# Odd mixer of a two-layer diffusion backbone: decays of head 0 under the query products, output gates by Exp and Ln, gate tiles between the values

## The chip, the cores and the metric

The kernel runs on one core of one Trainium2 chip. The metric is the device time of one execution in microseconds (us), lower is better. A core has TensorE (matrix products, PE in the profile, with its weight loads as PEld), VectorE (DVE), ScalarE (ACT), GpSimd (POOL), SyncE (SP, which issues most loads here) and 16 DMA engines. The engines run apart from each other and wait for each other by semaphores; each executes its own instructions in the order in which the program lists them.

## The reference, cut to what matters

Two layers; each is a SwiGLU FFN, a token mixer and a second FFN. 256 context tokens and 256 latent tokens of width 1024 pass through the same weights. The mixer of the second (odd) layer is a bidirectional gated linear attention (GLA) with 4 heads. Only its latent output is needed, since it is the last layer.

```python
def odd_mixer(hx, hc, w_in, w_out, w_gate, b_gate, norm_g, need_ctx):
    px = _split(hx @ w_in, ODD_SPLITS)     # q 512, k 512, v 1024, r 1024, low rank 32
    pc = _split(hc @ w_in, ODD_SPLITS)
    def heads(p):
        q = p[0].reshape(b, t, GLA_HEADS, GLA_K) * (GLA_K ** -0.5)
        ...
        lr_f, lr_b = jnp.split(p[4], 2, axis=-1)
        def decay(lr, d):
            z = (lr @ w_gate[d] + b_gate[d]).astype(jnp.float32)
            return (jax.nn.log_sigmoid(z) / GLA_TAU).reshape(b, t, GLA_HEADS, GLA_K)
        return (q, k, v), (decay(lr_f, 0),), (decay(lr_b, 1),)
    def merge(o, r):
        y = rms_norm(o, norm_g).reshape(b, t, -1) * jax.nn.silu(r)
        return y.astype(dt) @ w_out
    ...
    ox, oc = bidir_scan(gla_scan, qkv_x..., st0, need_ctx)   # chunks of 64, both directions
    return merge(ox, px[3]), ...
```

silu(r) = r * sigmoid(r) = r * exp(-ln(1 + exp(-r))).

## The kernel before, in words

**Products.** Weights come from HBM in fp32, 1 MB a load (a `raw` tile of 8 x 128 rows x 256 columns, three buffers, issued by SP). Each half of 128 columns is split by `split` into a high part `whi` (ScalarE, L122) and a low part `wlo` (VectorE, L123), two buffers of each. The activations are kept as `hh` and `hl` in the same manner. A product is then three matmuls (L148 high x high, L149 high x low, L150 low x high, in `mm3`) for each of 8 slices of the inner dimension. With 256 latent columns a half is 24 matmuls. `proj_fm` does this for keys, queries and output gates, with the features on the partitions, a PSUM bank `mm` per half (two banks in all), and an `emit` function that takes the result out of the bank. `proj_rows` makes the values of one head, with the tokens on the partitions: 96 matmuls (L636 to L638), both `mm` banks, and two copies by ScalarE (L640).

**The odd mixer** in program order: keys of all heads (`proj_first`); the eight tiles `sr` of the output gate, silu(r) (L1282, one ScalarE Silu per tile); the load of ScalarE's table for Ln and Exp (`table(LN_EXP)`, L109); `low_rank`, which makes the two 16-wide inputs `lr` of the decay gates; two pairs of queries (`q_pair`, L1122); the decays of head 0; then a loop over the heads. In the loop of head h come: the values of h (`proj_rows`); the scores of h (`scores`); the decays of head h + 1; the states of h (`states`); the output of h (`head_out`, which multiplies by `sr[2h]` and `sr[2h+1]`, L1273).

**`decays(h, d)`** for one head and one direction: a product `pz` of 512 columns (L1152); log sigmoid of it by a min and subtract on VectorE (L1155, L1159) and Abs, Exp, Ln on ScalarE (L1156 to L1158); two cumulative sums on VectorE (L1166 or L1172, L1169 or L1173); three Exp on ScalarE (L1178 to L1180); then products on VectorE: `kd` (L1182), `qe` (L1184), `ke` (L1185), `q2` (L1192), `ku` (L1198), `dec` (L1203); small copies on POOL; three transposes on TensorE (`ptg`, L1206 and L1207) and a copy `kt` (L1209).

**What sets the order on the engines.** The program is written in Tile. At build time a planner runs through the program with its own costs and gives each engine, at each time, the ready instruction that stands earliest in the program; a tile that must share a buffer waits until that buffer is free. So an engine's order is fixed before the run, and it isn't the written order: values of the next head, for instance, run on TensorE between the steps of the decays. On the chip each engine keeps to this order even when an instruction's input comes later than the planner thought.

Of the kernel before, what the change touches and what calls it, by code (L numbers as in the profile page):

```python
# [12 lines left out]
AF = mybir.ActivationFunctionType  # L13
ALU = mybir.AluOpType
# [15 lines left out]
LAT = slice(T, TT)  # L30
# [6 lines left out]
def backbone_kernel(  # L37
# [28 lines left out]
    nc = tc.nc  # L66
# [5 lines left out]
    def mm_bank(name):  # L72
        return pm.tile([P, 512], F32, tag="mm", name=name)
# [20 lines left out]
    one_t = cp.tile([P, 1], F32, name="one_t")  # L94
# [13 lines left out]
    def table(name):  # L108
        tc.keep_in_program_order(nc.scalar.preload_act_table_set(name))  # L109
# [4 lines left out]
    def load(view3):  # L114
        raw = wp.tile([P, 2048], F32, tag="raw", name="raw")
        a, b = view3.shape[1], view3.shape[2]
        r3 = raw[:, : a * b].rearrange("p (a b) -> p a b", a=a)
        nc.sync.dma_start(r3, view3)
        return r3
# [5 lines left out]
    def split(r3):  # L125
        a, b = r3.shape[1], r3.shape[2]
        hi = wp.tile([P, 1024], F32R, tag="whi", name="whi", bufs=2)
        lo = wp.tile([P, 1024], F32R, tag="wlo", name="wlo", bufs=2)
        hi3 = hi[:, : a * b].rearrange("p (a b) -> p a b", a=a)
        lo3 = lo[:, : a * b].rearrange("p (a b) -> p a b", a=a)  # L130
        split_into(hi3, lo3, r3)
        return hi3, lo3
# [8 lines left out]
    def rows(w, c0, n, k0=0, nk=KC):  # L141
        return w[k0 * P : (k0 + nk) * P, c0 : c0 + n].rearrange("(k p) n -> p k n", p=P)

    def half(r3, m):
        return split(r3[:, :, m * P : m * P + P])
# [6 lines left out]
    def gemm_h(ps, w, sl, at=None):  # L152
        at = at or sl
        for k in range(KC):
            wh, wl = (t[k] if isinstance(t, list) else t[:, k] for t in w)
            mm3(ps[:, sl], wh, wl, hh[k][:, at], hl[k][:, at], k == 0, k == KC - 1)
# [446 lines left out]
    def proj_fm(w, c0, n, emit, sl=BOTH):  # L603
        for mp in range(n // 2):
            r3 = load(rows(w, c0 + mp * 256, 256))
            for m in range(2):
                wt = half(r3, m)
                ps = mm_bank("ps_fm")
                gemm_h(ps, wt, sl)
                emit(2 * mp + m, ps)  # L610
# [13 lines left out]
    def proj_rows(w, c0, dst, col):  # L624

        r3 = load(rows(w, c0, 256))
        ps = [mm_bank("ps_v") for _ in range(2)]
        for i in range(2):
            wh, wl = split(r3[:, 4 * i : 4 * i + 4])
            for t in range(4):  # L630
                o = ps[t // 2][:, (t % 2) * T : (t % 2) * T + T]
                for k4 in range(4):
                    k = 4 * i + k4
                    ah, al = (a[k][:, t * P : t * P + P] for a in (hh, hl))

                    nc.tensor.matmul(o, lhsT=ah, rhs=wh[:, k4], start=k == 0 and t % 2 == 0, stop=False)  # L636
                    nc.tensor.matmul(o, lhsT=ah, rhs=wl[:, k4], start=False, stop=False)  # L637
                    nc.tensor.matmul(o, lhsT=al, rhs=wh[:, k4], start=False, stop=k == KC - 1 and t % 2 == 1)  # L638
        for a in range(2):
            nc.scalar.copy(dst[:, 2 * a : 2 * a + 2, col : col + T], ps[a].rearrange("p (t n) -> p t n", t=2))  # L640

    def out_split(k, src, sl):
        nc.scalar.copy(hh[k][:, sl], src)
        nc.vector.tensor_tensor(hl[k][:, sl], src, hh[k][:, sl].bitcast(F32), ALU.subtract)
# [18 lines left out]
    def out_weights(w, m0, spares):  # L663

        r = [load(rows(w, (m0 + 2 * a) * P, 256)) for a in range(2)]
        return [
            half(r[t // 2], t % 2) if sp is None else split_spare(r[t // 2], t % 2, sp) for t, sp in enumerate(spares)
        ]
# [6 lines left out]
    def taker(pool, slots, twice=()):  # L675
        slots = list(slots)

        def new():
            tag = slots.pop(0)
            return pool.tile([P, TT], F32R, tag=tag, name="wspare", bufs=2 if tag in twice else 1)  # L680

        return new
# [389 lines left out]
    def odd_mixer(nxt):  # L1072
        w_in, w_out = odd_w_in[0], odd_w_out[0]
# [10 lines left out]
        def t2k(tag, name, bufs=1):  # L1084
            return mp_.tile([P, TT], F32, tag=tag, name=name, bufs=bufs)
# [29 lines left out]
        sr = [mp_.tile([P, T], F32, name=f"sr{e}") for e in range(8)]  # L1115
# [3 lines left out]
        def q_pair(i):  # L1119
            proj_fm(  # L1120
                w_in, 256 * i, 2,
                lambda m, ps: nc.scalar.activation(qT[2 * i + m], ps[:, LAT], AF.Copy, scale=float(P) ** -0.5), LAT,  # L1122
            )

        def low_rank():

            for d in range(2):
                for i in range(3):
                    r0 = 32 * i + 16 * d
                    nc.sync.dma_start(wgraw[d][r0 : r0 + 16], gla_w_gate[0, d])  # L1130
                nc.scalar.copy(wg[d], wgraw[d])
                mid = slice(32, 64)
                nc.vector.tensor_tensor(wg[d][mid], wgraw[d][mid], wg[d][mid].bitcast(F32), ALU.subtract)
            lraw = mp_.tile([P, KC, 32], F32, name="lraw")
            nc.sync.dma_start(lraw, rows(w_in, 3072, 32))
            lw = wp.tile([P, 1024], F32R, tag="whi", name="lw", bufs=2)[:, 0:512].rearrange("p (k r) -> p k r", k=KC)
            nc.scalar.copy(lw[:, :, 0:32], lraw)
            nc.vector.tensor_tensor(lw[:, :, 32:64], lraw, lw[:, :, 0:32].bitcast(F32), ALU.subtract)
            psl = mm_bank("psl")
            for k in range(KC):  # L1140
                for i, a in enumerate((hh[k], hl[k])):
                    nc.tensor.matmul(psl[0:64], lhsT=lw[:, k], rhs=a, start=k + i == 0, stop=k + i == KC)
            low, s = t2k("la0", "low")[0:32], t2k("la1", "lrs")[0:32]
            nc.scalar.copy(low, psl[32:64])
            nc.vector.tensor_tensor(s, psl[0:32], low, ALU.add)
            nc.scalar.copy(lr[0:32], s)
            nc.vector.tensor_copy(lr[32:64], s)
            nc.vector.tensor_tensor(lr[64:96], s, lr[0:32].bitcast(F32), ALU.subtract)
# [95 lines left out]
        def states(h, d, kt, dec):  # L1244

            c0 = d
            hv = slice(h * T, h * T + T)
            pS = bank_d(d, "pSg")
            for t in range(2):
                nc.tensor.matmul(pS[:, :T], lhsT=kt[:, t * P : t * P + P], rhs=v[:, t, hv], start=t == 0, stop=t == 1)  # L1250
            nc.tensor.matmul(pS[:, T:], lhsT=kt[:, 2 * P : 3 * P], rhs=v[:, 2 + c0, hv], start=True, stop=True)
            st = mp_.tile([P, 2, T], F32, tag=f"st{d}", name="st", bufs=2)
            nc.scalar.copy(st[:, c0], pS[:, :T])
            nc.vector.scalar_tensor_tensor(st[:, 1 - c0], st[:, c0], dec, pS[:, T:], ALU.mult, ALU.add)
            return st
# [23 lines left out]
            lambda name: bank_d(0, name),  # L1279
            taker(mp_, ("la0", "la1", "ex0", "ex1", "kd0", "kd1", "spare", "ong")),  # L1280
        )
        proj_fm(w_in, 2048, 8, lambda m, ps: nc.scalar.activation(sr[m], ps[:, LAT], AF.Silu), LAT)  # L1282
        table(LN_EXP)
        low_rank()
        q_pair(0)
        q_pair(1)
        dirs = {0: [decays(0, d) for d in range(2)]}
        gate = md[:, 1, 40:48, :]
        st = STREAMS[1]

        def tiles(bank):

            p = [bank("ps_y") for _ in range(2)]
            return [p[t // 2][:, t % 2 * T : t % 2 * T + T] for t in range(4)]

        for h in range(4):
            proj_rows(w_in, 1024 + 256 * h, v, h * T)
            if h == 3:
                for k in range(4):
                    out_split(k, yo[k], LAST)  # L1300
                new = taker(mp_, [f"gk{i}" for i in range(4)] + ["la0", "la1", "ex0", "ex1"])
                ws = out_weights(w_out, 0, (None, None, new, new))
            am = scores(dirs[h])
            if h < 3:
                dirs[h + 1] = [decays(h + 1, d) for d in range(2)]
            sts = [states(h, d, *dirs[h][d][4:6]) for d in range(2)]
            head_out(h, am, [dirs[h][d][2] for d in range(2)], sts)
        ps = tiles(mm_bank)
# [10 lines left out]
        ps = tiles(bank_c)  # L1319
# [10 lines left out]
    with tc.tile_pool(name="plast", bufs=1, space=PSUM) as pa, tc.tile_pool(name="last", bufs=1) as fp:  # L1330

        def bank(name):
            return pa.tile([P, 512], F32, tag="ff", name=name, bufs=4)
# [27 lines left out]
        ps = [[bank("ps_l") for _ in range(2)] for _ in range(2)]  # L1361
# [94 lines left out]
```

## Time and profile before

| | us |
|---|---|
| median of 3 runs | 1787.75 (1784.91 to 1788.17) |
| the profiled execution | 1790.07 |
| its span, first to last instruction | 1788.4 |
| granted TensorE clock, mean | 0.995 |
| keys' last product, first of the gates | about 1440.9 |
| gate products (`sr`) | 1440.9 to 1463.9 |
| low rank, queries | 1463.7 to 1479.2 |
| head 0's decays beside its values | 1479.2 to 1493.8 |
| loops of heads 0 to 3, with outputs | 1493.8 to 1571.1 |

Times in the profile are counted from the span's start. In a table of stretches each row gives the busy time of each engine in that stretch (number of instructions in brackets), then the granted clock of TensorE as a share of full speed. Matmuls are pipelined: one of 256 columns is recorded with 0.28 us, but the next starts 0.12 us later. In the timeline a row gives start, duration, engine, line, operation and tiles, and in square brackets the idle time ahead of it and what ended it.

### The profile page before, as it was taken

What the parts mean: (1) busy time and instruction counts of PE and PEld (TensorE: products, weight loads), DVE (VectorE), ACT (ScalarE), POOL (GpSimd) and SP (SyncE); (2) the same over time, 40 slices, a digit from 0 to 9 for tenths busy, and PEclk for the clock granted to TensorE, in tenths of its full rate; (3) what the DMA queues carried; (4) which work ended last, traced back from release to release, by engine and by line L of the source; (5) the groups of instructions that cost most, each with busy time, mean ns of one, the idle gap of its engine ahead of it and who ended that gap; (6) DMA issues with size and microseconds to landing.
All of it is one profiled execution on the core that took longest, in us unless ns stands there. A gap on an engine that the chain in (4) does not pass through costs nothing.

```text
span 1788.4 us, 24901 instructions
## 1 busy us (share of the span) xinstructions
PE 1748.8 (98%) x10087; PEld 1505.4 (84%) x10087; DVE 1151.9 (64%) x1678; ACT 742.8 (42%) x1286; POOL 106.7 (6%) x172
## 2 busy tenths in 40 slices
PE   7999999999999999999999999999999999999998
PEld 5788888899887798888888898888888998889996
DVE  4677776657668866777753485777533737855555
ACT  3422222247558854222222252222322645654443
POOL 1000000003011111000000010000000200010000
PEclk9999999999999999999999999999999999999999
DMA  9555555544121214455543344555442632236553
GB/s 288 189 166 187 188 165 188 171 130 126 48 71 48 95 48 141 165 187 187 188 149 96 126 146 165 188 189 188 143 149 85 190 118 72 80 109 198 187 195 118
DMA packets 209303, 262.30 MB, mean 147 GB/s; under 512 B 6863, under 2 KB 188662, under 8 KB 209188
## 3 DMA queue, kind: packets, MB, share of 16 engines
q1 hardware_dynamic: 208160, 259.28, 44.4%
q8 instruction: 79, 1.29, 0.3%
q0 software_dynamic: 576, 0.84, 0.2%
q10 hardware_dynamic: 452, 0.59, 0.1%
q14 instruction: 36, 0.29, 0.0%
HBM read 259.64 MB, written 1.05 MB: 146 GB/s over the span
## 4 chain that ended last, share of the span: by engine, by line
PE 84%; DVE 8%; ACT 4%; issue 2%; DMA 2%; POOL 0%; SPq 0%; ACTq 0%; POOLq 0%; DVEq 0%
PE ps_ab L148 15%; PE ps_ab L149 15%; PE ps_ab L150 15%; PE ps_y L148 7%; PE ps_y L150 7%; PE ps_y L149 7%; PE ps_fm L150 2%; PE ps_fm L149 2%; PE ps_fm L148 2%; DVE wlo L123 2%; PE po L911 1%; ACT whi L122 1%; PE ada_ps L193 1%; PE ps_l L1386 1%; PE ps_l L1387 1%
## 5 line engine op out<-in xcount | busy, mean ns | idle before, releaser
L122 ACT CAST whi<-raw 128x1024 fp32r<-128x1024 f32 (+1 forms) x326 | 336.3, 1032 | 824.3 <-PE ps_ab L149 451.2
L123 DVE TENSOR_TENSOR wlo<-raw,whi 128x1024 fp32r<-128x1024 f32 (+1 forms) x326 | 392.5, 1204 | 305.9 <-ACT whi L122 301.3
L149 PE MATMUL ps_ab<-hl,whi 128*128 128x512 f32 (+1 forms) x1360 | 483.6, 356 | 2.6 <-POOL hl L279 2.3
L148 PE MATMUL ps_ab<-hh,whi 128*128 128x512 f32 (+1 forms) x1360 | 484.4, 357 | 1.7 <-ACT whi L122 1.0
L150 PE MATMUL ps_ab<-hh,wlo 128*128 128x512 f32 (+1 forms) x1360 | 482.5, 355 | 1.2 <-DVE wlo L123 1.1
L181 DVE SCALAR_TENSOR_TENSOR acc<-raw_ada,cs,acc 128x1024 f32<-128x1024 f32 x224 | 276.5, 1280 | 48.2 <-DMA raw_ada<-in_ada_w_dram 48.1
L148 PEld LDWEIGHTS ps_ab<-hh,whi 128*128 128x128 f32 x1360 | 255.1, 188 | 44.3 <-ACT whi L122 6.6
L149 PEld LDWEIGHTS ps_ab<-hl,whi 128*128 128x128 f32 x1360 | 255.5, 188 | 39.8 <-POOL hl L279 2.9
L150 PEld LDWEIGHTS ps_ab<-hh,wlo 128*128 128x128 f32 x1360 | 255.4, 188 | 38.7 <-DVE wlo L123 1.8
L150 PE MATMUL ps_y<-gh,wlo 128*128 128x512 f32 (+1 forms) x660 | 229.9, 348 | 0.4
L148 PE MATMUL ps_y<-gh,whi 128*128 128x512 f32 (+1 forms) x660 | 230.0, 348 | 0.0
L149 PE MATMUL ps_y<-gl,whi 128*128 128x512 f32 (+1 forms) x660 | 228.8, 347 | 0.0
L150 PEld LDWEIGHTS ps_y<-gh,wlo 128*128 128x128 f32 x660 | 124.9, 189 | 17.6 <-DVE wlo L123 1.5
L148 PEld LDWEIGHTS ps_y<-gh,whi 128*128 128x128 f32 x660 | 124.9, 189 | 17.0 <-ACT whi L122 1.2
L149 PEld LDWEIGHTS ps_y<-gl,whi 128*128 128x128 f32 x660 | 124.9, 189 | 15.5
L353 DVE TENSOR_TENSOR s<-ps_ab,s 128x512 f32<-128x512 f32 (+1 forms) x88 | 54.7, 622 | 118.0 <-PE ps_ab L150 117.9
L260 POOL TENSOR_TENSOR ssum<-ssum,sq 128x256 f32<-128x256 f32 x25 | 26.2, 1049 | 1103.0 <-ACT sq L258 834.4
L148 PE MATMUL ps_fm<-hh,whi 128*128 128x256 f32 (+1 forms) x256 | 83.9, 328 | 0.0
L150 PE MATMUL ps_fm<-hh,wlo 128*128 128x256 f32 (+1 forms) x256 | 83.5, 326 | 0.0
L149 PE MATMUL ps_fm<-hl,whi 128*128 128x256 f32 (+1 forms) x256 | 83.1, 325 | 0.0
L636 PE MATMUL ps_v<-whi,hh 128*128 128x256 f32 x256 | 74.2, 290 | 1.2 <-ACT mv L640 1.2
L637 PE MATMUL ps_v<-wlo,hh 128*128 128x256 f32 x256 | 74.6, 291 | 0.0
(375 smaller groups left out, 2396.3 us busy)
## 6 DMA issues: line engine op xcount, KB each, us to landing
raw<-in_ffn_w_in_dram SPq DMA_DIRECT2D x84, 1024.0 KB, 5.4
raw_ada<-in_ada_w_dram SPq DMA_DIRECT2D x64, 1024.0 KB, 5.0
raw<-in_ffn_w_out_dram SPq DMA_DIRECT2D x41, 1024.0 KB, 4.9
raw<-in_even_w_in_dram SPq DMA_DIRECT2D x12, 1024.0 KB, 5.4
raw<-in_odd_w_in_dram SPq DMA_DIRECT2D x12, 1024.0 KB, 5.5
raw<-in_ffn_w_out_dram SPq DMA_DIRECT2D x15, 768.0 KB, 4.2
raw_c<-in_ada_w_dram SPq DMA_DIRECT2D x16, 512.0 KB, 7.0
raw<-in_even_w_out_dram SPq DMA_DIRECT2D x4, 1024.0 KB, 5.0
```

The costliest lines, as they stand in the source:

```text
L122: nc.scalar.copy(hi3, r3)
L123: eng.tensor_tensor(lo3, r3, hi3.bitcast(F32), ALU.subtract)
L148: nc.tensor.matmul(ps, lhsT=wh, rhs=ah, start=first, stop=False)
L149: nc.tensor.matmul(ps, lhsT=wh, rhs=al, start=False, stop=False)
L150: nc.tensor.matmul(ps, lhsT=wl, rhs=ah, start=False, stop=last)
L181: nc.vector.scalar_tensor_tensor(ada_acc[i], r3[:, k2], s, ada_acc[i], ALU.mult, ALU.add)
L193: nc.tensor.matmul(ps[32 * j : 32 * j + 32, :256], lhsT=unit_e[:, 2 * (n - first) + i], rhs=acc[i][:, j * 256 : j * 256 + 256], start=n == ...
L260: (nc.gpsimd if i and k < KC - 2 else nc.vector).tensor_tensor(ssum[i][0], ssum[i][0], sq, ALU.add)
L353: nc.vector.tensor_tensor(s[:, sl], ps[1][:, sl], s[:, sl], ALU.mult)
L636: nc.tensor.matmul(o, lhsT=ah, rhs=wh[:, k4], start=k == 0 and t % 2 == 0, stop=False)
L637: nc.tensor.matmul(o, lhsT=ah, rhs=wl[:, k4], start=False, stop=False)
L911: nc.tensor.matmul(po[:, t], lhsT=w[:, kt, (t % 2) * P : (t % 2) * P + P], rhs=v[:, kt, h * P : h * P + P], start=kt == 0, stop=kt == nk - 1,)
```

## The change

The eight gate tiles lose their place after the keys. `emit_sr` makes silu without the Silu table: min(-r, 80) on VectorE, then Exp, Ln(1 + .), Exp(-.) on ScalarE in place, and a last product with r on VectorE, which reads r from the PSUM bank once more. `sr_pair(h)` projects the two tiles of head h. The pair of head 0 comes after the queries, the pair of head h + 1 between the values and the scores of head h. The decays of head 0 are moved ahead of the second pair of queries (they need only the first), and `low_rank` and the load of the Ln and Exp table now follow the keys directly.

```diff
@@ -1122,6 +1122,18 @@
+        def emit_sr(m, ps):
+
+            x, y = ps[:, LAT], sr[m]
+            nc.vector.tensor_scalar(y, x, -1.0, 80.0, ALU.mult, ALU.min)
+            nc.scalar.activation(y, y, AF.Exp)
+            nc.scalar.activation(y, y, AF.Ln, bias=one_t)
+            nc.scalar.activation(y, y, AF.Exp, scale=-1.0)
+            nc.vector.tensor_tensor(y, x, y, ALU.mult)
+
+        def sr_pair(h):
+            proj_fm(w_in, 2048 + 256 * h, 2, lambda m, ps: emit_sr(2 * h + m, ps), LAT)
+
@@ -1279,12 +1291,12 @@
-        proj_fm(w_in, 2048, 8, lambda m, ps: nc.scalar.activation(sr[m], ps[:, LAT], AF.Silu), LAT)
         table(LN_EXP)
         low_rank()
         q_pair(0)
+        dirs = {0: [decays(0, d) for d in range(2)]}
         q_pair(1)
-        dirs = {0: [decays(0, d) for d in range(2)]}
+        sr_pair(0)
         gate = md[:, 1, 40:48, :]
         st = STREAMS[1]
@@ -1295,6 +1307,8 @@
         for h in range(4):
             proj_rows(w_in, 1024 + 256 * h, v, h * T)
+            if h < 3:
+                sr_pair(h + 1)
             if h == 3:
```

## The prediction

> **What bounds the kernel now.** I read the page first (busy shares, loads), then a table of stretches through the odd mixer, TensorE's waits there, and last the timeline of the engines around the moved steps.
>
> ```profile
> span 1788.4 us, 24901 instructions
> ...
> PE 1748.8 (98%) x10087; PEld 1505.4 (84%) x10087; DVE 1151.9 (64%) x1678; ACT 742.8 (42%) x1286; POOL 106.7 (6%) x172
> ...
> raw<-in_odd_w_in_dram SPq DMA_DIRECT2D x12, 1024.0 KB, 5.5
> ```
>
> TensorE is busy 98% of the span. So an edit counts only by what it does to TensorE's idle time. The profiled execution took 1790.07 us for a span of 1788.4; the median of the runs is 1787.75. I work out a difference from rows of that execution and add it to the median. A difference under 0.2% (3.6 us) is about what a measurement of this kernel can't tell from none.
>
> The stretches below are the output gates (`sr`), head 0 (from its decays to its scores), and the loops of heads 0, 1 and 2. Columns: stretch, its length, busy time of each engine, granted clock, DMA.
>
> ```profile
> core 0: us, PE busy (x) PEld busy (x) DVE busy (x) ACT busy (x) POOL busy (x), PEclk, DMA share, GB/s
> 1440.90:1463.90 23.00, 23.00 (x192) 22.94 (x192) 7.78 (x7) 10.62 (x17) 0.00 (x0) 1.00 0.44 133
> 1479.20:1493.80 14.60, 13.28 (x106) 12.53 (x105) 13.03 (x24) 9.11 (x16) 1.80 (x6) 1.00 0.33 103
> 1493.80:1517.90 24.10, 22.85 (x156) 19.98 (x155) 16.91 (x35) 13.63 (x28) 1.73 (x6) 1.00 0.14 44
> 1517.90:1538.70 20.80, 19.89 (x146) 18.13 (x145) 17.41 (x38) 12.17 (x29) 2.39 (x6) 1.00 0.17 51
> 1538.70:1560.00 21.30, 20.50 (x151) 18.79 (x150) 20.59 (x45) 15.03 (x35) 1.74 (x6) 1.00 0.23 78
> ```
>
> ```profile
> PE ptg L1206 <- DVE kd L1182: 2.6, 5, 0.8
> PE po L1264 <- ACT st L1253: 1.3, 2, 0.8
> PE pt_o L1271 <- DVE on L1267: 0.3, 1, 0.3
> ```
>
> The gates are TensorE without a gap: 23.00 of 23.00 us, eight halves of 2.88 us. From head 0 to the loop of head 2 it is idle 1.32 + 1.25 + 0.91 + 0.80 = 4.3 us, mostly before the transposes of `kd`. That is all the change can win. VectorE is the other busy engine there: 13.03 of 14.60 us beside head 0.
>
> **The change part by part.**
>
> *Gates by Exp and Ln.* One ScalarE instruction per tile becomes three, two VectorE instructions come new, and a table load falls away.
>
> ```profile
> L123 DVE TENSOR_TENSOR wlo<-raw,whi 128x1024 fp32r<-128x1024 f32 x6 | 7.4, 1225 | 15.8 <-ACT whi L122 15.8
> L122 ACT CAST whi<-raw 128x1024 fp32r<-128x1024 f32 x7 | 7.3, 1047 | 10.8 <-PE ps_fm L149 10.7
> L1282 ACT ACTIVATE sr<-ps_fm 128x256 f32<-128x256 f32 x7 | 2.7, 380 | 0.0
> L1282 ACT ACT_TABLE_LOAD x1 | 1.3, 1283 | 0.0
> ...
> L1231 DVE TENSOR_TENSOR am<-px,blk 128x256 f32<-128x256 f32 x4 | 1.7, 419 | 2.7 <-PE px L1219 2.7
> ```
>
> ScalarE: 24 x 0.38 - 8 x 0.38 - 1.28 = +4.8 us. VectorE: 16 x 0.42 = +6.7 us. TensorE's products stay the same. On the path the load is worth nothing: ScalarE was busy 10.62 of 23.00 us beside the gates and TensorE had no gap. Six tiles move between the values: with their six splits (6 x 1.23) and 12 x 0.42, VectorE has 67.9 + 12.4 = 80.3 us from head 0 to the end of loop 2, in a stretch that grows from 80.8 by six halves to 98.1 us. Its share falls from 84% to 82%, so it is no bound on the average.
>
> *PSUM banks.* The last product reads `ps`, so the bank is held through five steps, not one: bare 2 x 0.42 + 3 x 0.38 = 2.0 us instead of 0.38. Two banks `mm` serve halves of 2.88 us, so it fits if no engine is late. Ends: 0, and 1 us for each of four pairs if the steps queue for a split (1.23) of VectorE. I take 0, because the next user of a bank between values comes only after the second half and the scores.
>
> *Loads.* Four loads of `sr` move behind those of the queries, and two of them behind values. With 5.5 us to land, three `raw` buffers and 5.76 us of products or more for each, they stay hidden; no wait of TensorE in these stretches is on a DMA. If that cover went, the cost would be a whole 5.5 us. The small loads of `low_rank` are issued ahead of them in SP's queue, which only matters if a large one waited behind them; none is moved past anything else. The copies and memsets that `decays` puts on POOL move with it, to an engine that is busy 1.80 of 14.60 us.
>
> *The decays of head 0 under the second pair of queries.* This is the part that decides. Weights for a half go through two buffers `whi`/`wlo`; the split for a half starts when the half two before it ends.
>
> ```profile
> 1473.48 1.05 ACT L122 CAST whi<-raw 128x1024 fp32r<-128x1024 f32 x1 [1.61 <-PE ps_fm L149]
> ...
> 1474.56 1.23 DVE L123 TENSOR_TENSOR wlo<-raw,whi 128x1024 fp32r<-128x1024 f32 x1 [1.84 <-ACT whi L122]
> ```
>
> The cast starts at 1473.48, as a half has just ended and the next one begins (its row names a product of the old half as the releaser); the low part is there at 1475.79, 2.3 us later. Products follow each other by 23.00 / 192 = 0.12 us, a half has 24 of them, and only its third needs the low part: 2.88 + 0.24 = 3.1 us after the cast's start. The slack is 0.8 us. A half of the values has 48 products (5.76 us), so beside values the slack is 3.7 us. Before, the decays of head 0 ran beside values. Now they run beside halves of 2.88 us. This is what VectorE did:
>
> ```profile
> 1479.16 0.63 PE L1152 MATMUL pz<-lr,wg 96*128 96x512 f32 x2
> ...
> 1480.92 1.22 DVE L123 TENSOR_TENSOR wlo<-raw,whi 128x1024 fp32r<-128x1024 f32 x1
> 1483.03 0.69 DVE L1159 TENSOR_TENSOR la<-la,ex 128x512 f32<-128x512 f32 x1 [0.90 <-ACT ex L1158]
> ...
> 1483.55 0.72 ACT L1158 ACTIVATE ex<-ex,one_t 128x512 f32<-128x512 f32 x1
> ...
> 1486.37 1.03 ACT L122 CAST whi<-raw 128x1024 fp32r<-128x1024 f32 x1
> ...
> 1491.37 0.24 DVE L1203 TENSOR_TENSOR dec<-e 128x1 f32<-128x1 f32 x1
> 1491.54 1.21 DVE L123 TENSOR_TENSOR wlo<-raw,whi 128x1024 fp32r<-128x1024 f32 x1
> ```
>
> From 1483.03 to 1491.6 VectorE works on decays without a break. The split whose cast ended at 1487.40 waited 4.1 us for its low part, until 1491.54: what stands earlier in the program goes first. In the changed program the decays stand before the second queries and before `sr`, so they still win.
>
> Count from `pz` as zero. Before the change: the low part at 1480.92 is +1.8, the burst is +3.9 to +12.2, the late low part is +12.4 to +13.6. After it: `pz` takes 0.47, the third query half runs to +3.35, the fourth to +6.23. The fourth's split takes the place at +1.8 and is done at +3.0, in time for +3.6. The buffer for the first half of `sr` comes free at +3.35; ScalarE is in the decays until +5.1 (1484.27), so its cast ends about +6.2, inside the burst. Its low part then comes where the late one came, done at +13.6. TensorE starts that half at +6.23, and its third product waits from +6.47. It has nothing else: values have no buffer, scores need the decays. Idle: 13.6 - 6.5 = **7.1 us**. If VectorE took the low part as soon as the cast is done, it would be there at +7.4, and the idle time 0.9 us. Those are the ends. I take 7.1, since the row at 1491.54 shows a split losing to the same instructions.
>
> What that replaces: head 0's stretch is 14.60 us, for 96 products of the values at 0.12 (11.5) and `pz` (about 0.5). The other 2.6 us were six transposes of the decays and the waits for them. Both now fall into the idle time beside `sr`: **-2.6**.
>
> *The clock.* An idle TensorE of that length has a second price, which this trace shows in the even mixer.
>
> ```profile
> 450.00:453.50 3.50, 0.26 (x3) 0.05 (x1) 3.36 (x6) 0.92 (x1) 0.52 (x1) 0.90 0.00 0
> 453.50:457.00 3.50, 3.48 (x15) 3.29 (x16) 3.21 (x6) 1.08 (x5) 0.00 (x0) 0.50 0.00 0
> 457.00:459.60 2.60, 2.60 (x14) 2.60 (x14) 0.43 (x2) 2.60 (x10) 0.00 (x0) 0.50 0.00 0
> 459.60:463.00 3.40, 3.40 (x28) 3.31 (x28) 1.21 (x5) 2.73 (x7) 0.00 (x0) 1.00 0.02 5
> ...
> 453.52 1.12 PE L788 MATMUL pmt<-ident,t 128*128 128x128 f32 x4 [3.26 <-DVE t L785]
> ```
>
> After 3.26 us of idling the granted clock is 0.50 for 6.1 us (453.5 to 459.6): half of that, 3.0 us, is lost. Ends: 0, if the transposes in between keep the clock up, and 3.0. I take **3.0**, as the idle time here is twice as long as in that row. [...]
>
> *The loops.* The `sr` pairs stand ahead of the scores, so they run when values run out; the 0.3 us before `pt_o` goes. The waits on `kd` and `st` stay: values were at hand there too, and TensorE's order already had the transposes next. Ends: 0 and -3.0 us, all idle time of the three loops. I take -0.3.
>
> Sum: 7.1 - 2.6 + 3.0 - 0.3 = **+7.2 us**; 1787.75 + 7.2 = **1795.0 us** (1797.3 for an execution like the profiled one, 2.3 us above the median).
>
> **The rivals.**
> 1. *The low part slips in* (an earlier gap of VectorE, or the order the planner finds). For it: VectorE was idle 0.90 us right before 1483.03. Against: the cast isn't done by then. Idle 0.9 instead of 7.1 and no drop of the clock; of head 0's 2.6 us only the idle 1.32 go: 0.9 - 1.3 - 0.3 = -0.7 us, 1787.0. No change that can be told.
> 2. *The moved tiles fill the waits*: faster. Head 0's 1.32 us of idling go with none beside the gates, and in the loops `sr` halves stand where TensorE waited for `kd` and `st`: -1.3 - 3.0 = -4.3 us, 1783.4. For it: 2.6 + 1.3 us of such waits. Against: they are waits for results that come later than planned, not for want of products. It decides if the low part is there by +7.2, so that the idle time stays under 0.7 us (4.3 - 3.6), and the loops lose all their waits.
> 3. *Banks held too long*: each of the four pairs waits 1 us more, on top of the sum: 7.2 + 4 = +11.2, 1799.0. For it: 2.0 us bare of 2.88, with splits of 1.05 and 1.23 us on the same two engines.
>
> **How the numbers follow.** Likeliest case 0.52 (own range 1791 to 1798); rival 1 0.24; rival 2 0.14; rival 3 0.10. Slower: 0.52 + 0.10, less 0.05 for a smaller idle time that stays under 3.6 us: 0.57. Within 0.2%: 0.24 + 0.05 - 0.02 = 0.27. Faster: 0.14 + 0.02 = 0.16. The range takes in rivals 1 and 3 and leaves out most of rival 2: 1785 to 1799.5.
>
> **What would show it.** Right: in the stretch after the second query pair, TensorE waits once for several us on the low part (L150 on L123) in a half of `sr`, and the granted clock is about 0.5 behind it; the waits of `ptg` on `kd` fall from five to three or so; the stretch of head 0's values has no gap; no table load for the gates. Wrong: no wait over 1 us on the low part there (rival 1), waits on `kd` and `st` gone from the loops (rival 2), or products waiting on the last product of a gate tile (rival 3). The forecast fails most easily if the decays' ranking over the splits is not kept.

## The result, and the profile after

The changed kernel takes 1801.82 us (median of 4 runs, 1799.83 to 1803.47); the kernel before took 1786.33 us in the runs beside it. The ratio is 1.0084 (95% interval 1.0069 to 1.0099), so the change costs 15.5 us (interval 12 to 18). The prediction said +7.2 us, with a range up to 1799.5: right in direction, half the size, outside the range. The profiled execution took 1803.02 us, 12.95 us more than the one before. Of all runs below, one ran at a much lower granted clock (0.636, 2537.59 us, the profiled run of experiment 3): it is in no ratio, and its trace is not read.

First the head of the page of the changed kernel: the span, and busy time by engine.

```profile
span 1801.3 us, 24940 instructions
...
PE 1757.4 (98%) x10087; PEld 1511.3 (84%) x10087; DVE 1159.6 (64%) x1694; ACT 747.2 (41%) x1301; POOL 106.1 (6%) x172
```

The shares are as before. VectorE has 7.7 us more (the prediction: 6.7), ScalarE 4.4 (4.8). Neither difference is the loss. TensorE has the same 10087 instructions, yet 8.6 us more busy time, and 4.3 us more idle time make up the rest of the longer span. Where? TensorE's waits in the odd mixer of the changed kernel (total, times, longest):

```profile
PE ps_v L636 <- DVE sr L1132: 3.9, 3, 2.6
PE ptg L1218 <- DVE kd L1194: 3.1, 2, 2.1
PE po L1276 <- ACT st L1265: 0.9, 2, 0.5
```

The first row has no counterpart before: a product of the values (L636) that waits for the last step of a gate tile (L1132). The waits on `kd` are two, not five, but one of them is 2.1 us long. The table of stretches of the changed kernel puts both in place. The first three rows are head 0's decays beside the second query pair and the first gate pair (site A); the next three are in the loop of head 2, just behind the last gate pair (site B).

```profile
core 0: us, PE busy (x) PEld busy (x) DVE busy (x) ACT busy (x) POOL busy (x), PEclk, DMA share, GB/s
1454.00:1459.70 5.70, 3.56 (x14) 2.21 (x12) 5.59 (x13) 3.44 (x8) 1.25 (x5) 0.72 0.21 72
1459.70:1463.00 3.30, 3.30 (x15) 2.72 (x15) 2.01 (x5) 0.00 (x0) 0.50 (x2) 0.50 0.01 2
1463.00:1469.70 6.70, 5.71 (x46) 5.50 (x44) 6.01 (x11) 3.66 (x8) 0.00 (x0) 0.97 0.50 151
1469.70:1481.90 12.20, 11.93 (x97) 11.73 (x98) 11.49 (x22) 8.67 (x17) 1.65 (x6) 1.00 0.29 91
...
1487.70:1505.90 18.20, 18.12 (x132) 17.21 (x131) 7.13 (x15) 6.00 (x14) 0.00 (x0) 1.00 0.29 93
...
1511.70:1533.50 21.80, 21.37 (x146) 18.80 (x145) 16.01 (x31) 11.85 (x24) 1.72 (x6) 1.00 0.24 78
...
1541.40:1544.50 3.10, 0.48 (x9) 0.35 (x8) 3.10 (x7) 3.09 (x7) 0.10 (x1) 1.00 0.01 3
1544.50:1549.00 4.50, 3.50 (x11) 2.64 (x12) 3.85 (x10) 2.85 (x7) 0.85 (x3) 0.59 0.01 2
1549.00:1555.50 6.50, 5.92 (x15) 3.30 (x15) 5.43 (x12) 2.40 (x6) 0.75 (x2) 0.50 0.01 3
```

A row's length less its busy time is idle time; what the clock took is estimated from the granted clock of the rows (somewhat high, as the last section shows). Site A: 2.14 + 0.00 + 0.99 = 3.1 us idle, and 0.28 x 5.70 + 0.50 x 3.30 + 0.03 x 6.70 = 3.4 us by the clock (the clock was still 1.00 from 1454 to 1456, in the wait, and TensorE was busy while it was low, so the whole row counts); together 6.5 us. Site B: 2.62 + 1.00 + 0.58 = 4.2 us idle, and, since part of the idle time fell under the low clock, only the busy time counts: 0.41 x 3.50 + 0.50 x 5.92 = 4.4 us; together 8.6 us. The clock's 7.8 us are most of TensorE's longer busy time (8.6). The rest of the loops is better than before: 0.27 + 0.08 + 0.43 = 0.8 us idle up to the last gate pair. Before, these parts had 4.3 us (1.32 in head 0, 2.96 in the loops). So 6.5 + 8.6 + 0.8 - 4.3 = +11.6 us are found.

The whole difference to find is larger than the 12.95 us between the two profiled executions. The keys, on code that is the same, end at 1440.6 us in the profile before and at 1437.8 in this one. From there to the end of the heads' outputs (1571.1 and 1582.2) it is 130.5 us before and 144.4 after, with 931 TensorE instructions in both: 13.9 us more. Some 2.3 us of them are not placed, and behind the odd mixer another 1.8 us.

**Site A** is the step that the prediction rested on. The rows are of TensorE, VectorE and ScalarE in the changed kernel's timeline; L1171 and L1215 are the old L1159 and L1203, moved by the new lines.

```profile
1447.45 0.63 PE L1164 MATMUL pz<-lr,wg 96*128 96x512 f32 x2
...
1451.33 0.69 DVE L1171 TENSOR_TENSOR la<-la,ex 128x512 f32<-128x512 f32 x1 [0.90 <-ACT ex L1170]
...
1452.60 1.04 ACT L122 CAST whi<-raw 128x1024 fp32r<-128x1024 f32 x1
...
1456.34 0.52 PE L1218 MATMUL ptg<-ident,kd 128*128 128x128 f32 x2 [2.14 <-DVE kd L1194]
...
1460.43 0.15 DVE L1215 TENSOR_TENSOR dec<-e 128x1 f32<-128x1 f32 x1
1460.50 1.21 DVE L123 TENSOR_TENSOR wlo<-raw,whi 128x1024 fp32r<-128x1024 f32 x1
...
1463.02 0.53 PE L150 MATMUL ps_fm<-hh,wlo 128*128 128x256 f32 x1
```

The cast for the first gate half ended at 1453.64; its low part began at 1460.50, behind the burst, 6.9 us later. `pz` was at 1447.45, so the low part was done at 1461.71, at +14.3 (predicted +13.6), and the first product with it (L150) ran at 1463.02.

**Site B** was not in the sum. First TensorE, then VectorE and ScalarE, of the changed kernel:

```profile
1541.06 0.36 PE L636 MATMUL ps_v<-whi,hh 128*128 128x256 f32 x1
...
1544.53 0.39 PE L636 MATMUL ps_v<-whi,hh 128*128 128x256 f32 x1 [2.60 <-DVE sr L1132]
1544.75 0.60 PE L1274 MATMUL po<-gv,am 128*128 128x256 f32 x2
...
1555.04 0.58 PE L637 MATMUL ps_v<-wlo,hh 128*128 128x256 f32 x1
```

```profile
1540.01 0.42 DVE L1128 TENSOR_SCALAR sr<-ps_fm 128x256 f32<-128x256 f32 x1 [0.19 <-PE ps_fm L150]
1540.45 0.88 DVE L1285 SCALAR_TENSOR_TENSOR yo<-pt_o,vec,sr 128x256 f32<-128x256 f32 x2
...
1542.94 1.22 DVE L1178 TENSOR_TENSOR_SCAN ex<-la,rm 128x511 f32<-128x511 f32 x1
1544.08 0.40 DVE L1132 TENSOR_TENSOR sr<-ps_fm,sr 128x256 f32<-128x256 f32 x1
...
1553.77 1.22 DVE L123 TENSOR_TENSOR wlo<-raw,whi 128x1024 fp32r<-128x1024 f32 x1
...
1536.40 1.05 ACT L122 CAST whi<-raw 128x1024 fp32r<-128x1024 f32 x1 [0.53 <-PE ps_fm L149]
...
1540.91 0.41 ACT L1129 ACTIVATE sr<-sr 128x256 f32<-128x256 f32 x1
1541.21 0.62 ACT L1169 ACTIVATE ex<-ex 128x512 f32<-128x512 f32 x1
1541.73 0.50 ACT L1130 ACTIVATE sr<-sr,one_t 128x256 f32<-128x256 f32 x1
1542.13 0.71 ACT L1170 ACTIVATE ex<-ex,one_t 128x512 f32<-128x512 f32 x1
1542.74 0.41 ACT L1131 ACTIVATE sr<-sr 128x256 f32<-128x256 f32 x1
...
1543.99 0.53 ACT L1251 COPY am<-pcross 64x128 f32<-64x128 f32 x2
```

The last gate tile needs its bank from its products' end at 1540.0 to the end of L1132 at 1544.5: 4.5 us for five steps that take 2.0 us bare. Other work stands between them on both engines. On ScalarE the three steps (L1129 to L1131) share the time with Exp and Ln of head 3's decays (L1169, L1170) and end at 1543.15, 2.7 us after L1128 instead of 1.1. On VectorE the last step then stands behind a cumulative sum of 1.22 us, another 0.9 us. The next product of the values of head 3 could start at 1541.93 and waits 2.60 us for this bank.

This wait is easy to see, but by these rows it cost little. It holds back one product. The next instruction in TensorE's order is `po` (L1274), which needs `am`, and ScalarE's last copy into `am` (L1251) ended at 1544.52. The products after it need the low part. Its cast was done at 1537.45; the low part began at 1553.77, 16.3 us later, behind all the decays of head 3. From 1544.5 to 1555.0 TensorE has hardly more than transposes, states and outputs, at a clock of 0.59 and 0.50. So site B is the mechanism of site A once more.

### The profile page after: what moved, and what is told of

It reads as the page before. It is cut to its first block, busy times and chain, and to the rows that moved or that the text cites. A ratio compares the mean times of both kernels' runs of the same rounds, so it can differ in the third digit from the quotient of the medians.

```text
span 1801.3 us, 24940 instructions
## 1 busy us (share of the span) xinstructions
PE 1757.4 (98%) x10087; PEld 1511.3 (84%) x10087; DVE 1159.6 (64%) x1694; ACT 747.2 (41%) x1301; POOL 106.1 (6%) x172
## 4 chain that ended last, share of the span: by engine, by line
PE 84%; DVE 7%; ACT 5%; issue 2%; DMA 2%; POOL 0%; SPq 0%; ACTq 0%; POOLq 0%; DVEq 0%
PE ps_ab L148 15%; PE ps_ab L149 15%; PE ps_ab L150 15%; PE ps_y L148 7%; PE ps_y L150 7%; PE ps_y L149 7%; DVE wlo L123 2%; PE ps_fm L150 2%; PE ps_fm L149 2%; PE ps_fm L148 2%; ACT whi L122 1%; PE ps_v L637 1%; PE ps_v L638 1%; PE po L911 1%; PE ps_v L636 1%
## 5 line engine op out<-in xcount | busy, mean ns | idle before, releaser
L150 PE MATMUL ps_ab<-hh,wlo 128*128 128x512 f32 (+1 forms) x1360 | 483.5, 356 | 1.6 <-DVE wlo L123 1.6
L150 PEld LDWEIGHTS ps_ab<-hh,wlo 128*128 128x128 f32 x1360 | 256.1, 188 | 39.1 <-DVE wlo L123 2.2
L150 PE MATMUL ps_y<-gh,wlo 128*128 128x512 f32 (+1 forms) x660 | 230.1, 349 | 0.4
L150 PEld LDWEIGHTS ps_y<-gh,wlo 128*128 128x128 f32 x660 | 125.0, 189 | 17.7 <-DVE wlo L123 1.5
L150 PE MATMUL ps_fm<-hh,wlo 128*128 128x256 f32 (+1 forms) x256 | 83.9, 328 | 0.0
L636 PE MATMUL ps_v<-whi,hh 128*128 128x256 f32 x256 | 73.9, 289 | 5.1 <-DVE sr L1132 3.9
L638 PE MATMUL ps_v<-whi,hl 128*128 128x256 f32 x256 | 74.2, 290 | 0.0
```

Source lines behind the costliest of these rows:

```text
L150: nc.tensor.matmul(ps, lhsT=wl, rhs=ah, start=False, stop=last)
```

## The experiments

Two theories run through them. **S**: a low part (`wlo`) ranked behind a burst of decays leaves TensorE without a half. **B**: the gate tile's chain holds an `mm` bank for too long. **N** is neither: the bare extra work of the new gates. All ratios are against the kernel before, run beside each kernel.

**1. Early decays alone.** The kernel before, with the decays of head 0 ahead of the second query pair; gates by Silu in their old place.

```diff
         q_pair(0)
+        dirs = {0: [decays(0, d) for d in range(2)]}
         q_pair(1)
-        dirs = {0: [decays(0, d) for d in range(2)]}
```

> The kernel before with one edit: the decays of head 0 stand ahead of the second query pair; gates by Silu in their old place. Theory S (a weight split ranked behind the decays on VectorE leaves TensorE without its low part): the first half of head 0's values now takes the place that the first gate half had, its low part comes about 12 us after pz, TensorE idles some 5 to 7 us with its clock halved behind it: +4 to +8 us against before. Rival B (the gate's five steps hold a PSUM bank too long) and rival N (the added Exp/Ln work loads ScalarE and VectorE): none of that is in this kernel, so within 2 us of before.

Measured: 1788.36 against 1786.43 us, 1.0015 (1.0006 to 1.0025): +2 to +3 us (interval 1.1 to 4.5), at or under the low end of S; the time alone hardly tells it from B and N. But the site is there, as two stretches of this kernel show, with the first value product in the first:

```profile
1475.00:1481.70 6.70, 4.42 (x19) 2.76 (x17) 6.65 (x17) 3.81 (x9) 1.76 (x5) 0.83 0.22 75
1481.70:1486.00 4.30, 4.30 (x22) 4.16 (x22) 3.40 (x7) 0.00 (x0) 0.00 (x0) 0.50 0.01 4
```

But most of the 19 instructions in the first row are transposes and scores of head 0 and `pz` of head 1 (four are products of the last query half and of the values), work that the loops then need not do between waits. So S is right on the mechanism and too dear on the net: the early decays cost 2 to 3 us here.

**2. Only the decays put back.** The changed kernel, with that one line moved back behind `q_pair(1)`.

```diff
-        dirs = {0: [decays(0, d) for d in range(2)]}
         q_pair(1)
         sr_pair(0)
+        dirs = {0: [decays(0, d) for d in range(2)]}
```

> The changed kernel with the decays of head 0 moved back behind the queries and the first gate pair, just ahead of the loop. Theory S: the loss beside the first gate pair (about 6.5 us) goes, the one in head 2's loop (about 8.4 us) stays: +6 to +10 us against before. Rivals B and N: +13 to +16 us, as the changed kernel.

Measured: 1792.23 us, 1.0029 (1.0019 to 1.004). Two thirds of the loss go, some 5 us stay, just under S's range. In its trace site B has moved up to the loop of head 1, with the same wait, and the next low part again far behind:

```profile
1508.86 0.40 DVE L1132 TENSOR_TENSOR sr<-ps_fm,sr 128x256 f32<-128x256 f32 x1
...
1509.31 0.58 PE L636 MATMUL ps_v<-whi,hh 128*128 128x256 f32 x1 [2.60 <-DVE sr L1132]
...
1517.77 1.22 DVE L123 TENSOR_TENSOR wlo<-raw,whi 128x1024 fp32r<-128x1024 f32 x1
```

So site B doesn't come from the early decays; it belongs to gate pairs between values.

**3. The last gate pair early.** The changed kernel, with `sr_pair(3)` right behind `sr_pair(0)`.

```diff
         sr_pair(0)
+        sr_pair(3)
 ...
-            if h < 3:
+            if h < 2:
                 sr_pair(h + 1)
```

> The changed kernel with the last gate pair (head 3) projected right behind the first one, so that nothing stands between head 2's values and scores. Theory S: head 3's values get their split ahead of head 3's decays again, the loss in head 2's loop (about 8.4 us) goes, the one at the start stays: +5 to +9 us against before. Rival B: eight gate tiles hold banks as before, two pairs now back to back, so no less than the changed kernel: +14 us or more.

Measured: 1792.03 us, 1.0032 (1.0022 to 1.0043). Without that pair in the loop of head 2 the loss is about 5.7 us, in S's range: the pair was worth some 10 us where it stood. What its engines waited for is not shown.

**4. Splits ahead of the decays.** The changed kernel, with the splits ranked earlier by the planner, from the second query pair to the values of head 3.

```diff
-        split_into(hi3, lo3, r3)
+        with (tc.high_priority(offset=ahead[0]) if ahead[0] else ExitStack()): split_into(hi3, lo3, r3)
 ...
-        q_pair(1)
+        ahead[0] = 400; q_pair(1)
 ...
             if h == 3:
+                ahead[0] = 0
```

> The changed kernel, where the splits of the second queries, the gates and the values are given a rank ahead of the decays for the planner (nothing else differs). Theory S: both losses go, the gain in head 0's loop (3.2 us) stays: -5 to +1 us against before. Rivals B and N: bank holding and added work are all there, so the time is that of the changed kernel, +13 to +16 us, or worse if the splits only delay the decays.

Measured: 1790.47 us, 1.002 (1.0011 to 1.003). Site B is gone, and with it three quarters of the loss; 3.6 us stay, more than S gave it. They lie at site A: from 1453.00 to 1470.00 TensorE is idle for 1.8 us at a mean clock of 0.90, and 1.7 us of that are a wait for a bank (L636 on L1132).

**5. The new gates in the old place.** The kernel before, with the eight tiles by Exp and Ln where the Silu ones were.

```diff
-        proj_fm(w_in, 2048, 8, lambda m, ps: nc.scalar.activation(sr[m], ps[:, LAT], AF.Silu), LAT)
         table(LN_EXP)
+        for h in range(4):
+            sr_pair(h)
```

> Only the gate arithmetic of the change: eight gate tiles by Exp and Ln in the old place after the keys, decays and everything else as before. Theory S: the added work lies beside TensorE, and no decays run beside these halves: -1 to +2 us against before. Rival B: five steps hold a bank for over 2 us of each half of 2.88 us, so the tiles wait for banks: +3 us or more. Rival N (the added ScalarE and VectorE work itself costs): likewise +3 us or more.

Measured: 1786.89 against 1786.88 us, 1.0 (0.9991 to 1.0008). The arithmetic is free, and in a row of halves so is the bank. The groups of this kernel show that the price of a step is not what matters (busy total, mean ns):

```profile
L1128 DVE TENSOR_SCALAR sr<-ps_fm 128x256 f32<-128x256 f32 x8 | 3.4, 425 | 8.6 <-PE ps_fm L150 8.6
L1132 DVE TENSOR_TENSOR sr<-ps_fm,sr 128x256 f32<-128x256 f32 x8 | 3.4, 425 | 1.8 <-ACT sr L1131 1.1
```

Both steps take 0.42 us, as predicted. Here VectorE was waiting for the gate tile's product (8.6 us of idling ahead of L1128); in the loop of head 2 the chain's steps were queued behind other work. N falls.

**6. The bank freed at once.** The changed kernel, with the gate product copied out of its bank by ScalarE; the five steps read the copy.

```diff
-
-            x, y = ps[:, LAT], sr[m]
+            x, y = tp.tile([P, T], F32, tag="u", name="u", bufs=3), sr[m]
+            nc.scalar.copy(x, ps[:, LAT])
```

> The changed kernel, where ScalarE first copies each gate tile out of PSUM and the five steps work on the copy, so that a bank is held for one step again. Theory S: the 2.8 us in which head 2's loop waits for a bank go or turn into a longer wait for the low part of the split that is late behind the decays; the loss at the start stays: +11 to +15 us against before. Rival B: the loss in head 2's loop is the bank's, so all of it goes: +5 to +8 us.

Measured: 1791.09 us, 1.0024 (1.0015 to 1.0033): some 11 us better than the changed kernel, for eight copies more, and better than B itself had it. The low part for the values of head 3 now gets its place ahead of the burst of decays:

```profile
1539.22 1.22 DVE L123 TENSOR_TENSOR wlo<-raw,whi 128x1024 fp32r<-128x1024 f32 x1
1540.35 0.88 DVE L1285 SCALAR_TENSOR_TENSOR yo<-pt_o,vec,sr 128x256 f32<-128x256 f32 x2
1541.14 0.42 DVE L1132 TENSOR_TENSOR sr<-u,sr 128x256 f32<-128x256 f32 x1
```

Here are 26.62 us from the first product of the last gate pair on, with the bank freed:

```profile
1533.38:1560.00 26.62, 25.73 (x193) 23.83 (x192) 24.32 (x54) 21.34 (x52) 2.22 (x6) 1.00 0.24 80
```

And the same 26.62 us in the changed kernel:

```profile
1533.45:1560.07 26.62, 22.43 (x128) 17.97 (x127) 22.30 (x49) 17.13 (x42) 1.70 (x6) 0.81 0.19 63
```

193 TensorE instructions against 128: 65 at 0.12 us are an estimated 7.8 us, and that is site B. The held bank is a necessary part of it. Experiment 4 left the bank held and got rid of the site too. So neither half of the mechanism is enough alone. What both remedies change on the chip is the place of the low part in VectorE's order, ahead of the burst instead of behind it: the ranking does so directly, the free bank by way of the planner. Why the planner gave the low part at 1539.22 a place only when the bank was free is not shown by any view: its own times aren't in the trace. Site A is as it was: the low part of the first gate half begins at 1460.68, and TensorE's wait on `kd` is again 2.1 us. So the 4.3 us that stay are put down to it.

**7 and 8. Decays back, with splits first; and with the bank freed as well.** Edits 2 and 4 together, then 2, 4 and 6.

> The changed kernel with the decays of head 0 back behind the first gate pair and with the splits ranked ahead of the decays. Theory S: head 0 loses what it lost before (about 3.5 us in its 20 us), the loops lose 2 us less than before: -4 to +1 us against before. Rival B: the bank waits stay, +4 us or more.

> The kernel with decays back and splits first, and banks freed by a copy too. Theory S: as without the copy or up to 1 us less, -5 to +1 us against before. Rival B: clearly less than without the copy, by 2 us or more.

Measured: 1785.93 us, 0.9992 (0.9983 to 1.0), and 1785.59 us, 0.9996 (0.9985 to 1.0007). The loss is gone in both, and the copy adds nothing that can be told once the splits go first.

**9. Decays back and the bank freed, no ranking.** Edits 2 and 6.

> The changed kernel with the decays of head 0 back behind the second query pair, and with the gate product copied out of its PSUM bank first (one ScalarE copy, the five steps read the copy). No ranking of splits. Theory S+B (both sites of the changed kernel are needed for its +15 us: head 0's decays beside the short gate halves, 6 to 10 us, and a bank held by the gate tile's chain, 5 to 11 us): within -2 to +2 us of the kernel before. Rival L (loops lose time by the mere place of the gate pairs between the values, since each pair delays the scores): +4 us or more.

Measured: 1785.83 us, 0.9995 (0.9984 to 1.0005). The 15.5 us are gone without touching the ranking. TensorE's waits of this kernel on values and decays are short again:

```profile
PE ptg L1218 <- DVE kd L1194: 2.1, 3, 1.1
...
PE ps_v L637 <- DVE wlo L123: 0.8, 1, 0.8
```

Rival L falls: gate pairs between the values cost nothing by themselves.

With the changed kernel and experiments 2, 6 and 9 all four combinations are there. With the bank held, the early decays cost 15.5 - 5.2, some 10 us; with the bank freed, 4.3 + 0.9, some 5 us. So the two causes don't simply add up: about 5 us of the loss need both (each figure is good to 2 or 3 us).

**10. Early decays with both remedies.** Edits 4 and 6 in the changed kernel.

> The changed kernel with its decays of head 0 left early, but with both remedies: splits ranked ahead of the decays, and the gate product copied out of its bank. Theory S: what is left is head 0's site itself with the split no longer behind the decays, 0 to +3 us against the kernel before (+3.6 with the ranking alone, +4.2 with the copy alone). Rival A (the two remedies work on the same loss, so the second adds nothing): +3 to +4.5.

Measured: 1789.75 us, 1.0015 (1.0007 to 1.0024), +2.7 us. The low part of the first gate half is now in the middle of the burst:

```profile
1452.74 0.67 DVE L1181 TENSOR_TENSOR_SCAN binc<-rm,la 128x256 f32<-128x256 f32 x1
1453.32 1.20 DVE L123 TENSOR_TENSOR wlo<-raw,whi 128x1024 fp32r<-128x1024 f32 x1
1454.44 0.68 DVE L1194 TENSOR_TENSOR kd<-gk,ex 128x512 f32<-128x512 f32 x1
```

It is done at 1454.52, 7.2 us earlier than in the changed kernel. 2.7 us stay all the same: from 1447.40 to 1463.00 TensorE is still idle for 1.4 us, at a mean clock of 0.89. The intervals of this run and of experiments 4 and 6 overlap, so whether the two remedies add up at this site stays open (S and rival A are not told apart).

**11. Splits first, nothing else.** The kernel before, with edit 4 alone.

> The kernel before with nothing changed but the rank of the splits, from the second query pair to the values of head 3. Theory S: there the decays run beside values, whose halves of 48 products leave 3.7 us of slack, so a late low part costs little: -2 to +1 us. Rival K (the waits on kd in the loops are there because the splits come at the wrong time): a gain of 2 us or more.

Measured: 1783.74 against 1787.08 us, 0.998 (0.9972 to 0.9989): 3.6 us faster by the ratio, more than S gave. It is the fastest version of the study. TensorE's waits on `kd` went from 2.6 us in five to this:

```profile
PE ptg L1206 <- DVE kd L1182: 1.5, 4, 0.6
PE po L1264 <- ACT st L1253: 0.8, 1, 0.8
```

The two rows had 3.9 us together and have 2.3 now. So part of these waits hung on where the splits stood, as rival K had it; the other 2 us of the gain are not placed. The prediction had taken all but 0.3 us of the idle time in the loops to stay.

## Why the prediction was wrong, by its own steps

- *The low part behind the burst* (+7.1, less 2.6): right in mechanism. The low part was done 14.3 us after `pz` (13.6 predicted), in the half and behind the instructions named. "It has nothing else" was wrong: TensorE took scores of head 0 and `pz` of head 1 in the wait, since `kd` of the first direction was ready at 1456.28, before the burst ended. So the trace shows a wait on `kd` (2.14 us) and not one of L150 on the low part.
- *The clock* (+3.0): about right for site A, whose rows give 3.4 us. Site B's 4.4 us were not foreseen.
- *Site A with the loops*: site A lost 6.5 us, 5.2 more than head 0's idle time before, and the loops up to the last gate pair won 2.2 us of the 2.96 (predicted 0.3), so +3.0 net where the sum had +7.2. The early decays alone cost 2 to 3 us (experiment 1), and some 5 us beside the gate halves with the bank freed (experiment 6 against 9). This part was too dear.
- *PSUM banks* (0, ends 0 and 4): the step that failed. The reason given was that the next user of a bank between values comes only after the second half and the scores. In the loop of head 2 that cover was 1.9 us (1540.0 to 1541.9) against a chain that took 4.5 us. The chain was 2.0 us bare, and I did count that it could queue, but only behind a split, and not behind a head's decays. And I priced the wait alone. The wait is 2.6 us and by itself cost little; the held bank goes with an order of VectorE in which the low part of head 3's values stands behind the whole burst of head 3's decays. Site B is 8.6 us, and freeing the bank was worth 11 us.
- *The loops* (-0.3, ends 0 and -3.0) left that out too: the working gave halves of the values 3.7 us of slack and looked for a late low part only beside head 0. At site B the low part began 16.3 us after its cast was done.
- *Rival 3* named the waits for banks. They come to 3.9 us, beside its 4, but that is luck: it had 1 us at each of four pairs, where there was one long wait behind the last pair and 1.3 us behind the first, and it had no low part behind them.
- *Arithmetic, the table load, the loads* (0): right (experiment 5).
- *"Head 0's values without a gap"*: wrong, they waited for a bank too.

The two wrong sizes pointed in opposite directions, so the total looks nearer than the working was: that is luck.

## What to carry to other kernels

Where each engine's order is fixed at build time, price a chain that holds a PSUM bank by what else stands in its engines' queues between its steps, not by its bare sum, and copy the product out first if that is more than the cover. Then look at where the next weight split stands in its engine's order; here the visible wait for the bank cost little, and the late split behind it much. A weight split that feeds the busiest engine should rank ahead of long VectorE work that feeds nothing urgent; here that rank alone, without any other change, was worth 3.6 us. When the starved engine has other work, ask what it will do in the gap: the gap that was filled with later work in experiment 1 came back in part (by its two rows 2.28 us idle and 0.17 x 6.70 + 0.50 x 4.30 = 3.3 us by the clock, less head 0's 1.3 us before: an estimated 4.3 us at the site, 2 to 3 us in the time).

## What the runs showed of the hardware

The prediction took its clock term from a row of the kernel before: 3.26 us of idling, then 6.1 us at 0.50. The row ahead of that (450.00 to 453.50 us, at 0.90) holds an estimated 0.7 us more at the half clock (twice 0.10 x 3.50), so the clock fell some 2.5 us into the wait, and was low for some 6.8 us. In the changed kernel the idle time ahead of the fall was 2.14 us at site A (the row of 1456.34) and 2.60 us at site B, there followed by 0.8 us of work (from 1545 to 1546 us the clock was 0.65). By the clocks of the stretches the half clock then lasted 6.9 us at site A (twice 1.60 + 1.65 + 0.20 = 3.45) and 10.2 us at site B (twice 0.41 x 4.50 + 0.50 x 6.50 = 5.1), though TensorE was busy 3.30 of 3.30 us and 5.92 of 6.50 us in it: about as long as before at site A, and longer at site B. Transposes and single products ended neither stretch. What made the clock fall and what brought it back isn't told apart by these runs.

A half clock cost a little less than half of the time. In the kernel before, the value products from 455.29 to 457.00 us, at 0.50, follow each other by 0.21 us, against 0.12 us at 1.00: 0.09 of 0.21, some 0.44 of the time. By that measure the figures by the clock above (3.4 and 4.4 us, and the 3.0 us of the prediction) are high by about an eighth.
